# Summing the right operands T1 to T4 of two feed-forward networks from transposed token tiles

## The chip, the core and the metric

The kernel runs on one core of one Trainium2 chip. The metric is the device time of one execution in microseconds (us). Engine names in the profile: PE is TensorE (PEld its weight loads), DVE is VectorE, ACT is ScalarE, POOL is GpSimd, SP is SyncE, which here only issues DMAs. A difference of about 0.3% is what a measurement of this kernel can tell from none.

## The reference

One layer of a hybrid decoder, on 1024 tokens of 1024 channels, in float32:

```python
h = h + 0.5 * swiglu(rmsnorm(h, ffn1_norm), ffn1_w_gate, ffn1_w_up, ffn1_w_down)
...                                    # mixer: four mLSTM heads, eight attention heads
h = h + 0.5 * swiglu(rmsnorm(h, ffn2_norm), ffn2_w_gate, ffn2_w_up, ffn2_w_down)
...                                    # gated per-layer embedding
out = rmsnorm(h)

def swiglu(x, w_gate, w_up, w_down):   # w_gate, w_up: 1024 x 2816, w_down: 2816 x 1024
    return (jax.nn.silu(x @ w_gate) * (x @ w_up)) @ w_down
```

The change touches the first step of both networks: the normalized tokens, transposed, become the right operands of `x @ w_gate` and `x @ w_up`.

## The kernel before

Tokens are handled in eight tiles of 128. Each float32 product is made of three products of a rounded part (`hi`) and a rest (`lo`), in a format that TensorE takes at full rate; `split_from` (line 100) makes both: ScalarE casts the source to `hi`, VectorE subtracts `hi` from the source to get `lo`.

`x @ w_gate` and `x @ w_up` are made by pairs of 128 output columns, as 2 x 2 blocks in Winograd's form: seven block products instead of eight, each of 12 matmuls of 128x512. For this, x transposed is cut in four blocks of 512 channels by 512 tokens: B11 and B21 are the two halves of the channels for the first 512 tokens (tiles 0 to 3), B12 and B22 those for the last 512 (tiles 4 to 7). The right operands are B11, B21, B22 and four sums: T1 = B12 - B11, T2 = B22 - T1, T3 = B22 - B12, and T4 = T2 - B21 with its sign turned. The order of the products in the first pair of columns is g1 u1 g2 u2 g5 g3 u5 u3 g6 g7 g4 u6 u7 u4 (g for gate, u for up): 1 takes B11, 2 B21, 5 T1, 3 B22, 6 T2, 7 T3, 4 T4.

`wino_normer` (line 174) takes one token tile after another. `step(i)` normalizes tile i (a square with a row sum on ScalarE at line 114, a small step on VectorE and GpSimd, and a scaling of 128x1024 on VectorE at line 117) and then calls `finish` for the tile before. For tiles 0 to 3 `finish` transposes both halves with four TensorE transposes each into a PSUM tile (`wino_put`, line 162) and splits them into B11 and B21. The rows of these tiles are kept for tiles 4 to 7: in the first network in SBUF (tag `xk`, four buffers), in the second in DRAM (`xnD`, stored at line 193, loaded at line 196). For tiles 4 to 7 `finish` transposes B22's part, forms the sums on untransposed rows (line 209, two of them on GpSimd, two on VectorE), transposes T1's part, and stores T2, T3 and T4, still as rows, in DRAM (`tD`, line 218). In the second network the two transposes of a tile use PSUM tiles `tr` (two buffers), in the first `pt`, which share five PSUM buffers with the products `pp`.

After the last tile, `ffn` (line 516) loads T2, T3 and T4 (line 546, 1 MB each) into the places of their `lo` parts. Then `wino_rest` (line 222) runs once between products: after the product g3 for T2, after u5 for T3, after u3 for T4. It transposes 16 blocks of 128x128 into four PSUM tiles and splits them. Next come the products that use T2, T3 and T4.

In the first network the token tiles are taken between products of `p @ w_ple_proj` (an order written out as a string at line 1390); in the second, inside the product with `w_out` (`out_f`, line 1288), one tile for every 24 matmuls. Weights are prepared (loaded, summed, split) by `prep` up to three products ahead, and all DMAs go through the queue of SP in order. Within each engine, the order of the instructions is laid out by a scheduler when the kernel is built; it need not be that of the source.

Of the kernel before, what the change touches and what calls it, by code (L numbers as in the profile page):

```python
# [9 lines left out]
F32 = mybir.dt.float32  # L10
# [14 lines left out]
# pairs of dff tiles, and the order of the seven block products of a Winograd form  # L25
# [4 lines left out]
class Net:  # L30
# [26 lines left out]
    def raw_cols(self, w, c0):  # L57
        """128 columns of a [1024, N] weight: row k * 128 + p at [p, k]."""
        r = self.rp.tile([P, KT, P], F32, tag="raw", name="raw")
        self.nc.sync.dma_start(out=r, in_=w[:, c0:c0 + P].rearrange("(k p) n -> p k n", p=P))  # L60
        return r
# [6 lines left out]
    def split(self, raw, pool=None, tag="w", aside=False):  # L68
        """raw = hi + lo, both in float32r."""
# [7 lines left out]
    def split2(self, raw, aside=False):  # L77
        """The two halves of k of a weight tile, each (hi, lo)."""
        return [self.split(raw[:, 4 * j:4 * j + 4, :], aside=aside) for j in range(2)]
# [13 lines left out]
    def mm3(self, out, ahi, alo, bhi, blo, first, last):  # L93
        """out (+)= a.T @ b with a = ahi + alo and b = bhi + blo."""
# [5 lines left out]
    def split_from(self, hi, lo, src, aside=False):  # L100
        """src (PSUM or SBUF) = hi + lo; aside: on GpSimd (SBUF only)."""
# [8 lines left out]
    def norm_rows(self, src, gain, dst):  # L110
        """dst = RMSNorm(src) * gain for 128 tokens; dst also takes the squares."""
# [7 lines left out]
    def xunit(self):  # L119
        """Four k tiles by 512 columns, (hi, lo)."""  # L120
        return tuple(self.xp.tile([P, 4, 512], F32R, tag=t, name=t) for t in ("xhi", "xlo"))

    def new_xt(self):
        """[half of the tokens][half of the k tiles] -> (hi, lo)"""
        return [[self.xunit() for _ in range(2)] for _ in range(2)]

    def normer(self, src, gain, dst):
        """RMSNorm of one token tile after another, transposed and split into dst(i) -> (hi, lo).
        Returns step(i), which takes token tile i and finishes the one before; step.rows(i) only takes it,
        step.next() only finishes the oldest."""  # L130
# [31 lines left out]
    def wino_put(self, B, name, rows, i):  # L162
        """512 columns of token tile i, transposed, into a right operand."""
# [6 lines left out]
        c = (i % 4) * P  # L170
        hi, lo = B[name]
        self.split_from(hi[:, :, c:c + P], lo[:, :, c:c + P], pt)

    def wino_normer(self, src, gain, B, rows, bufs):
        """RMSNorm of one token tile after another into the right operands of the seven products
        (x transposed: rows k < 512 and k >= 512, columns t < 512 and t >= 512, Winograd's form).
        Three operands wait in DRAM for wino_rest. step(i) takes token tile i and finishes the one
        before, step.last() finishes the last."""
# [3 lines left out]
        def step(i):  # L182
            if i < 4 and bufs[2]:
                xn = rows.tile([P, D], F32, tag="xk", name="xn", bufs=bufs[2])
# [7 lines left out]
            elif i < 4 and not kept:  # L192
                nc.sync.dma_start(out=self.xnD[:, i, :], in_=xn)
# [7 lines left out]
        def finish():  # L201
            i, xn, o = queue.pop(0)
            a, b = xn[:, 0:512], xn[:, 512:1024]
            if i < 4:
                self.wino_put(B, "B11", a, i)
                self.wino_put(B, "B21", b, i)
                return
            oa, ob = o[:, 0:512], o[:, 512:1024]
            sub = lambda d, x, y, e=nc.vector: e.tensor_tensor(out=d, in0=x, in1=y, op=ALU.subtract)
            t3 = rows.tile([P, 512], F32, tag="t3", name="t3", bufs=bufs[1])  # L210
            self.wino_put(B, "B22", b, i)
            sub(t3, b, a, nc.gpsimd)
            sub(a, a, oa)
            self.wino_put(B, "T1", a, i)
            sub(oa, b, a)
            sub(ob, ob, oa, nc.gpsimd)
            for n, t in enumerate((oa, t3, ob)):
                nc.sync.dma_start(out=self.tD[:, n, i - 4, :], in_=t)
# [3 lines left out]
    def wino_rest(self, B, name):  # L222
        """One of the operands that wait in DRAM, through its place for lo."""
        hi, lo = B[name]
        pts = []
        for i in range(4):
            pts.append(B["ps"].tile([P, 512], F32, tag="pp", name="pt", bufs=5).rearrange("p (a b) -> p a b", a=4))
            for j in range(4):
                self.nc.tensor.transpose(pts[i][:, j, :], lo[:, i, j * P:(j + 1) * P].bitcast(F32), self.ident)
        for i, pt in enumerate(pts):  # L230
            self.split_from(hi[:, :, i * P:i * P + P], lo[:, :, i * P:i * P + P], pt)

    def swiglu(self, B, w_gate, w_up, pools):
        """hidD = silu(x @ w_gate) * (x @ w_up), transposed, by pairs of dff tiles; the products of a
        pair (2 x 2 blocks: dff tile, half of k, half of the tokens) in Winograd's form with seven
        block products, each of three float32r products."""
# [3 lines left out]
        def pair(m, which, s):  # L240
            """Appends the seven products of the dff tiles m, m + 1."""
# [13 lines left out]
            # the first pair's tile a is loaded again for the sums  # L255
# [18 lines left out]
            def slot(r, c):  # L274
                """Where block (dff tile r, token half c) is put together."""
# [7 lines left out]
            def out(r, c, x, y, t):  # L283
                """Block (r, c) is x + y."""
# [8 lines left out]
            def hidden(r, c):  # L293
                """The left operands of the product with w_down: A11 = H00, A12 = H10, A21 = H01, A22 = H11
                (H: dff tile, half of the tokens), S1 = A21 + A22, S2 = S1 - A11, S3 = A11 - A21, S4 = A12 - S2."""
# [1215 lines left out]
```

## Time and profile before

| What | Value |
|---|---|
| Median of 3 runs | 2029.75 us (2027.75 to 2033.62) |
| Span of the profiled execution | 2033.1 us |
| Time of the profiled execution | not given beside its span |
| TensorE busy | 1982.7 us, 98% of the span |
| VectorE busy | 1408.4 us, 69% |
| ScalarE busy | 856.9 us, 42% |
| GpSimd busy | 135.9 us, 7% |
| DMA | 252.62 MB, mean 124 GB/s |
| The first network's token tiles and first products | 0 to 85 us of the span |
| The same of the second network | 1240 to 1320 us |

A median of the runs is a time of the whole execution; the span goes from the first to the last instruction of one profiled execution, 3.35 us more than the median here. Busy times are sums over the whole span, so an engine's share says little on one stage; the windows and timelines further down show the two stages.

### The profile page before, as it was taken

Reading aid. Unit: us, or ns where it says so; the run is one execution under the profiler, and the core shown is the slowest. Engines: PE = TensorE matmul, PEld = TensorE weight load, DVE = VectorE, ACT = ScalarE, POOL = GpSimd, SP = SyncE. Lnnn points to the kernel's source line nnn. Section 1 sums busy time; section 2 is a strip of 40 time slices with the busy share of each in tenths; the row PEclk is TensorE's granted clock in tenths of the full one; section 3 lists DMA queues with packets and bytes.
Section 4 is the critical chain, followed back from the end, with each engine's and each line's share of the span. In section 5 each row is a group of like instructions: output and inputs, shape, how many; then the busy total and the mean of one; then the engine's idle time right before and its main releaser. Section 6 shows DMA issues by size and latency. Waiting matters only on the chain. (4 is left out here: it accounts for less than half of the span.)

```text
span 2033.1 us, 25588 instructions
## 1 busy us (share of the span) xinstructions
PE 1982.7 (98%) x9251; PEld 1618.8 (80%) x9251; DVE 1408.4 (69%) x2425; ACT 856.9 (42%) x1634; POOL 135.9 (7%) x148
## 2 busy tenths in 40 slices
PE   7999999999999999999999999999999999999998
PEld 6788888888888787788788777788888888888786
DVE  6966766777877683655565665877777777886766
ACT  6433333334445443435565642433333333444443
POOL 2000000000000110121110411100000000000011
PEclk9999999999999999999999999999999999999999
DMA  7623322338432331122112538533223237633422
GB/s 284 207 89 104 112 96 95 104 112 310 149 101 99 111 86 53 42 95 53 53 54 78 190 122 289 197 106 112 94 94 124 89 99 243 234 104 102 131 70 86
DMA packets 205359, 252.62 MB, mean 124 GB/s; under 512 B 12632, under 2 KB 138096, under 8 KB 204464
## 3 DMA queue, kind: packets, MB, share of 16 engines
q1 hardware_dynamic: 205232, 250.99, 37.8%
q8 instruction: 72, 1.18, 0.2%
q14 instruction: 55, 0.45, 0.1%
HBM read 172.18 MB, written 74.58 MB: 121 GB/s over the span
## 5 line engine op out<-in xcount | busy, mean ns | idle before, releaser
L96 PE MATMUL pp<-xhi,whi 128*128 128x512 f32 x704 | 275.6, 391 | 0.5 <-DVE s L272 0.5
L98 PE MATMUL pp<-xhi,wlo 128*128 128x512 f32 x704 | 274.1, 389 | 0.8 <-DVE wlo L103 0.8
L97 PE MATMUL pp<-xlo,whi 128*128 128x512 f32 x704 | 274.7, 390 | 0.0
L102 ACT CAST whi<-raw 128x512 fp32r<-128x512 f32 x180 | 111.3, 621 | 257.4 <-PE pp L97 177.2
L102 ACT CAST whi<-S 128x512 fp32r<-128x512 f32 x176 | 109.5, 622 | 240.8 <-PE pp L97 186.2
L96 PE MATMUL dn<-xhi,whi 128*128 128x512 f32 x528 | 205.7, 390 | 0.1
L97 PE MATMUL dn<-xlo,whi 128*128 128x512 f32 x528 | 205.5, 389 | 0.0
L98 PE MATMUL dn<-xhi,wlo 128*128 128x512 f32 x528 | 205.1, 389 | 0.0
L102 ACT CAST whi<-ar 128x512 fp32r<-128x512 f32 x132 | 82.3, 623 | 183.3 <-PE dn L97 174.8
L98 PEld LDWEIGHTS pp<-xhi,wlo 128*128 128x128 f32 x704 | 132.3, 188 | 29.2 <-DVE wlo L103 1.2
L96 PEld LDWEIGHTS pp<-xhi,whi 128*128 128x128 f32 x704 | 132.3, 188 | 29.1 <-DVE s L272 0.8
L97 PEld LDWEIGHTS pp<-xlo,whi 128*128 128x128 f32 x704 | 132.3, 188 | 27.7 <-DVE xlo L103 0.3
L103 DVE TENSOR_TENSOR wlo<-raw,whi 128x512 fp32r<-128x512 f32 x162 | 110.5, 686 | 59.7 <-ACT whi L102 46.7
L103 DVE TENSOR_TENSOR wlo<-S,whi 128x512 fp32r<-128x512 f32 x176 | 120.1, 682 | 25.8 <-ACT whi L102 25.7
L103 DVE TENSOR_TENSOR wlo<-ar,whi 128x512 fp32r<-128x512 f32 x132 | 90.7, 687 | 63.9 <-ACT whi L102 63.8
L96 PEld LDWEIGHTS dn<-xhi,whi 128*128 128x128 f32 x528 | 99.1, 188 | 21.0 <-DVE t L272 0.5
L98 PEld LDWEIGHTS dn<-xhi,wlo 128*128 128x128 f32 x528 | 99.1, 188 | 20.7
L97 PEld LDWEIGHTS dn<-xlo,whi 128*128 128x128 f32 x528 | 99.1, 188 | 20.6
L272 DVE TENSOR_TENSOR p<-pp,p 128x512 f32<-128x512 f32 x88 | 60.6, 689 | 74.9 <-PE pp L98 74.9
L107 POOL TENSOR_TENSOR r<-v,mhalf 128x1 f32<-128x1 f32 (+1 forms) x56 | 43.9, 784 | 909.6 <-DVE v L116 756.1
L96 PE MATMUL pj<-xhi,whi 128*128 128x512 f32 x248 | 102.6, 414 | 0.1
L97 PE MATMUL pj<-xlo,whi 128*128 128x512 f32 x248 | 97.5, 393 | 0.0
(350 smaller groups left out, 4515.0 us busy)
## 6 DMA issues: line engine op xcount, KB each, us to landing
ar<-hidD SPq DMA_DIRECT2D x60, 512.0 KB, 3.6
hidD<-t SPq DMA_DIRECT2D x110, 256.0 KB, 3.4
raw<-in_ffn_w_gate_dram SPq DMA_DIRECT2D x46, 512.0 KB, 3.9
raw<-in_ffn_w_up_dram SPq DMA_DIRECT2D x46, 512.0 KB, 3.7
raw<-in_w_in_dram SPq DMA_DIRECT2D x24, 512.0 KB, 3.9
hidD<-x SPq DMA_DIRECT2D x44, 256.0 KB, 3.1
ar<-hidD SPq DMA_DIRECT2D x32, 256.0 KB, 2.9
w<-in_ffn_w_down_dram SPq DMA_DIRECT2D x8, 1024.0 KB, 11.1
```

Of the source, the lines that this page charges most:

```text
L96: mm(out, ahi, bhi, start=first, stop=False)
L97: mm(out, ahi, blo, start=False, stop=False)
L98: mm(out, alo, bhi, start=False, stop=last)
L102: self.nc.scalar.copy(out=hi, in_=src)
L103: (self.nc.gpsimd if aside else self.nc.vector).tensor_tensor(out=lo, in0=src, in1=hi.bitcast(F32), op=ALU.subtract)
L107: self.nc.gpsimd.tensor_tensor(out=r, in0=v, in1=self.mhalf[:, :v.shape[-1]], op=ALU.pow)
L272: add = lambda d, x, y: nc.vector.tensor_tensor(out=d, in0=x, in1=y, op=ALU.add)
```

## The change

`wino_normer` now transposes both halves of every token tile first (`turned`, in place of `wino_put`). For tiles 0 to 3 B11 and B21 are split from the transposed tiles in PSUM as before, and ScalarE also copies both to SBUF, over the normalized rows; it is these transposed tiles that are kept, and in the second network stored in `xnD`, now in `finish`. For tiles 4 to 7 T1 and T2 are formed on VectorE from PSUM and the kept tiles, T3 (as T2 - B11) and T4 on GpSimd from SBUF. T1 is split from SBUF. T2, T3 and T4 go to DRAM already transposed, T2 from the tile of the normalized rows, in pieces of 128 columns (512 bytes) instead of rows of 512 (2 KB). `wino_rest` has no transposes any more; it splits the loaded operand in place, in four blocks of 512 columns. The tag `t3` and its buffer are gone, so `bufs` has one entry less.

```diff
-    def wino_put(self, B, name, rows, i):
+    def turned(self, B, rows):
         if "ps" in B:
             pt = B["ps"].tile([P, 512], F32, tag="pp", name="pt", bufs=5).rearrange("p (a b) -> p a b", a=4)
         else:
             pt = self.tr()
         for j in range(4):
             self.nc.tensor.transpose(pt[:, j, :], rows[:, j * P:(j + 1) * P], self.ident)
-        c = (i % 4) * P
-        hi, lo = B[name]
-        self.split_from(hi[:, :, c:c + P], lo[:, :, c:c + P], pt)
+        return pt
...
         def step(i):
-            if i < 4 and bufs[2]:
-                xn = rows.tile([P, D], F32, tag="xk", name="xn", bufs=bufs[2])
+            if i < 4 and bufs[1]:
+                xn = rows.tile([P, D], F32, tag="xk", name="xn", bufs=bufs[1])
                 kept.append(xn)
...
-            elif i < 4 and not kept:
-                nc.sync.dma_start(out=self.xnD[:, i, :], in_=xn)
             elif i >= 4:
                 o = self.rp.tile([P, D], F32, tag="raw", name="xo")
                 nc.sync.dma_start(out=o, in_=self.xnD[:, i - 4, :])
...
         def finish():
             i, xn, o = queue.pop(0)
-            a, b = xn[:, 0:512], xn[:, 512:1024]
+            c = (i % 4) * P
+            put = lambda name, src: self.split_from(B[name][0][:, :, c:c + P], B[name][1][:, :, c:c + P], src)
+            quad = lambda t, b: t[:, b * 512:b * 512 + 512].rearrange("p (a c) -> p a c", a=4)
+            pa = self.turned(B, xn[:, 0:512])
+            pb = self.turned(B, xn[:, 512:1024])
+
+            a, b = quad(xn, 0), quad(xn, 1)
             if i < 4:
-                self.wino_put(B, "B11", a, i)
-                self.wino_put(B, "B21", b, i)
+                put("B11", pa)
+                put("B21", pb)
+                nc.scalar.copy(out=a, in_=pa)
+                nc.scalar.copy(out=b, in_=pb)
+                if not bufs[1]:
+                    nc.sync.dma_start(out=self.xnD[:, i, :], in_=xn)
                 return
-            oa, ob = o[:, 0:512], o[:, 512:1024]
+            oa, ob = quad(o, 0), quad(o, 1)
             sub = lambda d, x, y, e=nc.vector: e.tensor_tensor(out=d, in0=x, in1=y, op=ALU.subtract)
-            t3 = rows.tile([P, 512], F32, tag="t3", name="t3", bufs=bufs[1])
-            self.wino_put(B, "B22", b, i)
-            sub(t3, b, a, nc.gpsimd)
-            sub(a, a, oa)
-            self.wino_put(B, "T1", a, i)
-            sub(oa, b, a)
-            sub(ob, ob, oa, nc.gpsimd)
-            for n, t in enumerate((oa, t3, ob)):
-                nc.sync.dma_start(out=self.tD[:, n, i - 4, :], in_=t)
+            sub(a, pa, oa)
+            put("B22", pb)
+            sub(b, pb, a)
+            put("T1", a)
+            sub(oa, b, oa, nc.gpsimd)
+            sub(ob, ob, b, nc.gpsimd)
+            for n, t in enumerate((b, oa, ob)):
+                nc.sync.dma_start(out=self.tD[:, n, :, c:c + P], in_=t)
...
     def wino_rest(self, B, name):
         hi, lo = B[name]
-        pts = []
-        for i in range(4):
-            pts.append(B["ps"].tile([P, 512], F32, tag="pp", name="pt", bufs=5).rearrange("p (a b) -> p a b", a=4))
-            for j in range(4):
-                self.nc.tensor.transpose(pts[i][:, j, :], lo[:, i, j * P:(j + 1) * P].bitcast(F32), self.ident)
-        for i, pt in enumerate(pts):
-            self.split_from(hi[:, :, i * P:i * P + P], lo[:, :, i * P:i * P + P], pt)
+        for k in range(4):
+            self.nc.scalar.copy(out=hi[:, k, :], in_=lo[:, k, :].bitcast(F32))
+            self.nc.vector.tensor_tensor(out=lo[:, k, :], in0=lo[:, k, :].bitcast(F32), in1=hi[:, k, :].bitcast(F32), op=ALU.subtract)
...
-        N.ffn(h, ffn1_norm[0], ffn1_w_gate[0], ffn1_w_up[0], ffn1_w_down[0], norms, hook, (3, 1, 4), True)
+        N.ffn(h, ffn1_norm[0], ffn1_w_gate[0], ffn1_w_up[0], ffn1_w_down[0], norms, hook, (3, 4), True)
...
-    N.ffn(h, ffn2_norm[0], ffn2_w_gate[0], ffn2_w_up[0], ffn2_w_down[0], norms, hook, (2, 1, 0), release=late.close)
+    N.ffn(h, ffn2_norm[0], ffn2_w_gate[0], ffn2_w_up[0], ffn2_w_down[0], norms, hook, (2, 0), release=late.close)
```

The rest of the diff takes comments and docstrings out of the source, with the lines kept, and changes no instruction.

## Rows read from the trace of the kernel before

**Rows 1.** The page's first part: busy us, share of the span and instructions of each engine (PE is TensorE, PEld its weight loads, DVE VectorE, ACT ScalarE, POOL GpSimd).

```profile
PE 1982.7 (98%) x9251; PEld 1618.8 (80%) x9251; DVE 1408.4 (69%) x2425; ACT 856.9 (42%) x1634; POOL 135.9 (7%) x148
```

**Rows 2.** Busy time by stretches of 10 us, at the start of the first feed-forward network (two) and of the second (one). In order: the stretch in us from the span's start, its length, and for each engine the busy us and in brackets its instructions; then the granted clock of TensorE as a share of full speed, the busy share of the DMA engines, and GB/s.

```profile
60.00:70.00 10.00, 7.71 (x40) 5.74 (x39) 8.23 (x14) 4.66 (x9) 0.00 (x0) 1.00 0.90 335
...
70.00:80.00 10.00, 10.00 (x62) 8.70 (x61) 9.48 (x17) 6.14 (x12) 0.00 (x0) 1.00 0.37 113
...
1290.00:1300.00 10.00, 8.30 (x37) 6.56 (x35) 7.99 (x14) 4.45 (x7) 0.00 (x0) 1.00 1.00 351
```

**Rows 3.** TensorE's timeline at the start of the first network. Columns of a timeline: start in us, duration in us (of all instructions merged into the row, if several), engine, line, operation, output and input by the program's names, tile, how many instructions, and in square brackets the idle time of that engine just before, with what ended it.

```profile
51.61 2.34 PE L169 MATMUL pt<-ident,xn 128*128 128x128 f32 x16
...
57.58 0.50 PE L97 MATMUL pp<-xlo,whi 128*128 128x512 f32 x1
...
61.96 0.50 PE L98 MATMUL pp<-xhi,wlo 128*128 128x512 f32 x1 [0.80 <-DVE wlo L103]
...
64.12 0.39 PE L98 MATMUL pp<-xhi,wlo 128*128 128x512 f32 x1
...
66.00 1.94 PE L229 MATMUL pt<-ident,T2lo 128*128 128x128 f32 x16 [1.48 <-DMA T2lo<-tD]
...
75.03 1.91 PE L229 MATMUL pt<-ident,T4lo 128*128 128x128 f32 x16
...
76.70 0.48 PE L96 MATMUL pp<-T2hi,whi 128*128 128x512 f32 x1
...
82.38 0.40 PE L96 MATMUL pp<-T4hi,whi 128*128 128x512 f32 x1
```

**Rows 4.** TensorE's timeline at the start of the second network, columns as in rows 3.

```profile
1286.71 0.66 PE L169 MATMUL pt<-ident,xn 128*128 128x128 f32 x4 [0.78 <-DVE xn L209]
...
1297.92 0.39 PE L98 MATMUL pp<-xhi,wlo 128*128 128x512 f32 x1
...
1300.30 3.25 PE L229 MATMUL pt<-ident,T2lo 128*128 128x128 f32 x16 [1.99 <-DMA T2lo<-tD]
...
1312.67 0.48 PE L96 MATMUL pp<-T2hi,whi 128*128 128x512 f32 x1
...
1318.35 0.40 PE L96 MATMUL pp<-T4hi,whi 128*128 128x512 f32 x1
```

**Rows 5.** A stretch of 2 us in the second network, columns as in rows 2.

```profile
1302.00:1304.00 2.00, 2.00 (x10) 1.90 (x9) 1.23 (x3) 1.47 (x3) 0.00 (x0) 0.50 0.23 68
```

**Rows 6.** VectorE's timeline in the first network, columns as in rows 3.

```profile
50.03 1.42 DVE L209 TENSOR_TENSOR xn<-xn 128x512 f32<-128x512 f32 x2 [1.41 <-POOL t L209]
...
55.64 1.89 DVE L103 TENSOR_TENSOR xlo<-pt,xhi 128x512 fp32r<-128x512 f32 x3 [0.60 <-ACT xhi L102]
...
67.70 2.48 DVE L103 TENSOR_TENSOR T2lo<-pt,T2hi 128x512 fp32r<-128x512 f32 x4 [1.19 <-PE pt L229]
...
72.32 2.48 DVE L103 TENSOR_TENSOR T3lo<-pt,T3hi 128x512 fp32r<-128x512 f32 x4 [0.34 <-ACT T3hi L102]
...
77.12 2.48 DVE L103 TENSOR_TENSOR T4lo<-pt,T4hi 128x512 fp32r<-128x512 f32 x4
```

**Rows 7.** Groups of VectorE's instructions from 56 to 80 us, one row for a line, names and shape: count, busy us, mean ns of one, and idle time before them with what ended it.

```profile
L252 DVE TENSOR_TENSOR S<-S,raw 128x512 f32<-128x512 f32 x4 | 2.8, 688 | 0.6 <-DMA raw<-in_ffn_w_gate_dram 0.3 <-DMA raw<-in_ffn_w_up_dram 0.3
...
L252 DVE TENSOR_TENSOR S<-raw 128x512 f32<-128x512 f32 x4 | 2.7, 685 | 0.3 <-DMA raw<-in_ffn_w_up_dram 0.3
```

**Rows 8.** VectorE's timeline in the second network, columns as in rows 3.

```profile
1297.08 0.69 DVE L252 TENSOR_TENSOR S<-S,raw 128x512 f32<-128x512 f32 x1 [1.14 <-DMA raw<-in_ffn_w_up_dram]
...
1303.00 2.48 DVE L103 TENSOR_TENSOR T2lo<-pt,T2hi 128x512 fp32r<-128x512 f32 x4 [0.77 <-ACT T2hi L102]
...
1308.17 2.48 DVE L103 TENSOR_TENSOR T3lo<-pt,T3hi 128x512 fp32r<-128x512 f32 x4 [0.32 <-ACT T3hi L102]
...
1313.02 2.47 DVE L103 TENSOR_TENSOR T4lo<-pt,T4hi 128x512 fp32r<-128x512 f32 x4
```

**Rows 9.** Timelines of the first network, one row of GpSimd and two of VectorE (the normalization of a token tile, beside a GpSimd subtraction and without one), columns as in rows 3.

```profile
30.05 1.28 POOL L209 TENSOR_TENSOR t<-xn 128x512 f32<-128x512 f32 x1
...
30.12 2.28 DVE L117 SCALAR_TENSOR_TENSOR xn<-h,r,gain 128x1024 f32<-128x1024 f32 x1 [1.92 <-POOL r L107]
...
25.93 1.28 DVE L117 SCALAR_TENSOR_TENSOR xn<-h,r,gain 128x1024 f32<-128x1024 f32 x1
```

**Rows 10.** DMA issues: output and input, engine, how many, KB of each, median us from issue to landing.

```profile
ar<-hidD SPq DMA_DIRECT2D x60, 512.0 KB, 3.6
...
raw<-in_ffn_w_gate_dram SPq DMA_DIRECT2D x46, 512.0 KB, 3.9
...
tD<-xn SPq DMA_DIRECT2D x8, 256.0 KB, 4.1
...
tD<-xo SPq DMA_DIRECT2D x8, 256.0 KB, 2.2
```

**Rows 11.** ScalarE's copies of 128x512 from PSUM to SBUF in the first 60 us (count, then minimum, median and maximum ns), and a stretch of 30 us with the columns of rows 2.

```profile
L599 ACT COPY pp<-pp x16: 586/600/639, 14.2 to 48.2; 128x512 f32<-128x512 f32 x16
...
20.00:50.00 30.00, 28.10 (x145) 22.79 (x144) 21.81 (x33) 20.53 (x42) 11.56 (x11) 1.00 0.74 267
```

**Rows 12.** Timeline rows of the second network: TensorE's transposes of token tile 4, and ScalarE's squares of token tile 6. Columns as in rows 3.

```profile
1265.32 1.03 PE L169 MATMUL tr<-ident,xn 128*128 128x128 f32 x8
...
1273.85 1.06 ACT L114 ACTIVATE xn<-h 128x1024 f32<-128x1024 f32 x1 [0.83 <-DMA tD<-t]
```

## The prediction

> **What bounds the kernel now.** I read the page's first part first, then the stretches around the two places that the change touches: the start of the first feed-forward network (FFN1, up to 85 us of the span) and of the second (FFN2, 1240 to 1320 us). TensorE is busy 98% of the span [rows 1], so what is worth something here is TensorE's own work and the few waits of TensorE, and nothing that another engine does beside it.
>
> The windows show the three places where that is not so. From 60 to 70 us TensorE has 7.71 busy us of ten, and from 1290 to 1300 us 8.30; VectorE (DVE) has 9.48 from 70 to 80 us, as TensorE has 10.00 [rows 2]. So right behind the stall DVE is nearly full too, and a faster TensorE may find DVE in its way. That is the point on which my sum turns.
>
> TensorE's timeline shows the stall itself. In FFN1 the last matmul of a product starts at 64.12; the 16 transposes of T2 wait 1.48 us more for the load of T2 and start at 66.00; those of T4 start at 75.03 and the next product, the first that uses T2, at 76.70 [rows 3]. FFN2 has the same: 1297.92, a wait of 1.99, 1300.30, and the first product with T2 at 1312.67; there the last tile's T1 transposes waited 0.78 for DVE besides [rows 4]. After the wait of 1.99 the granted clock was 0.50 (1.2 GHz) from 1302 to 1304 [rows 5], which is why those 16 transposes took 3.25 us.
>
> **What goes.** Per network 3 x 16 = 48 transposes in wino_rest (8 per token tile stay). Sixteen take 75.03 to 76.70 = 1.67 us [rows 3], so 96 take 10.0 us of TensorE. With them goes TensorE's wait for the load: the two products that run between the loads (u5, u3) no longer have transposes ahead of them. The ceiling is read from the gap. In FFN1 12.35 us lie between the end of the product at 64.35 (64.12 + 0.23) and the first with T2; two products take 82.38 - 76.70 = 5.68; 6.7 us can go. In FFN2 (1312.67 - 1298.15) - 5.68 = 8.8, and 0.78 for T1. Together 16.3 us.
>
> **What DVE lets through.** The twelve subtractions per network that make the lo parts of T2, T3 and T4 stay: four take 2.48 us [rows 6], from PSUM before and from SBUF after, and SBUF sums of the same size have the same 0.69 us mean [rows 7]. Before, the last of T4 ends at 77.12 + 2.48 = 79.60 and T4's first product starts at 82.38: 2.8 us to spare. In FFN2 1313.02 + 2.47 = 1315.49 against 1318.35: 2.9 [rows 3, 4, 6, 8]. If DVE came no earlier, 2.8 and 2.9 would be all that TensorE gains. DVE comes earlier by idle time that it now has. In FFN2 that is 1.14 + 0.77 + 0.32 = 2.2 us, the second of which is the wait for the old transposes [rows 8]; so 2.9 + 2.2 + 0.8 (T1) = 5.9. In FFN1 0.6 + 0.3 (waits for weights) [rows 7] and 0.34 [rows 6] give 2.8 + 1.2 = 4.0. The 1.19 before T2's first subtraction I don't count: T2's data landed at 66.0 before, and it lands no sooner after, so cast and subtraction start near 67 anyway. The ends: DVE blocks all but the 2.8 and 2.9, or nothing, since DVE can take T4 before sums that are needed later.
>
> **What moves behind the transposes.** B12 - B11 (T1) and B22 - T1 (T2) were DVE work on rows, done before TensorE reached the tile: both of the last pair of sums at 50.03 [rows 6], the transposes at 51.61 [rows 3]. Now both wait for the transposes. In FFN1 the lo part of T1's last tile ends at 55.64 + 1.89 = 57.53 [rows 6] and the product's second matmul starts at 57.58 [rows 3]: nothing to spare. After: the first eight of the 16 transposes end near 52.6; then eight DVE operations of two tiles (8 x 0.62 = 5.0) and two others (1.2) end at 58.8, that is 1.3 late. GpSimd comes on top. It has the same two subtractions per tile, but both now depend on T2 and start just when DVE makes T1's lo part from SBUF. The rows show what that does: DVE's normalization took 2.28 us beside a GpSimd subtraction that started 0.07 before it, 1.28 without one [rows 9]. So 0 to 1.3 us for each of two tiles; I take the middle, 1.3. Of 2.6 us TensorE's 0.80 wait at 61.96 [rows 3] takes up some; 1.8 stay. FFN1: 4.0 - 1.8 = 2.2.
>
> The page SBUF — State Buffer of the Trainium skill (Who interferes with whom) says that a DVE instruction with two SBUF inputs and a GpSimd instruction that reads SBUF exclude each other for the whole instruction, and that one with an input in PSUM is not touched. By that rule both T1 subtractions pay in full or stop GpSimd, and FFN1 gives 0.9, not 2.2; the trace agrees with the rule where it has such a pair (2.28 against 1.28).
>
> In FFN2 T1's last lo part is less pressed: two products of B21 (5.7 us) run between the last tile's transposes and T1's first use, in FFN1 only one. DVE's count there is the same, so I charge nothing; without that cover it would be FFN1's 1.8. T3 was ready early before and is not now; its load follows T2's instead of leading it, which costs nothing as long as T3 lands 2.8 us after T2, and a megabyte took less than that at the rates of these windows (335 to 351 GB/s: 3.0 us, all but equal) [rows 2]. I take zero there, 1 us at worst.
>
> **What is added.** ScalarE copies each of the first four transposed tiles to SBUF: 8 x 0.60 = 4.8 us per network [rows 11]. In FFN1 ScalarE is busy 20.5 of the 30 us from 20 to 50 [rows 11], so they fit; but they hold the PSUM buffers longer, and TensorE waited for such buffers there. 0 to 2 us, I take 0.4, near zero since TensorE has other work between tiles. The tD stores have pieces of 512 bytes, not 2 KB. Weights come in such pieces: 512 KB land in 3.9 us, the 2-KB pieces of hidD in 3.6 [rows 10]. By that an eighth more for 256 KB that took 4.1, some 0.4 us, hidden in FFN2 by the products and inside the 67 us above in FFN1. The xnD store of FFN2 waits for the copies now, one tile later, with the load of the next h row behind it on the SP queue; it waited for a normalization before, which ends about when the tile before it has been transposed and copied, so zero, and 1 us for the six tiles at worst.
>
> **Sum.** 2.2 + 5.9 - 0.4 = 7.7 us off the profiled span of 2033.1, which gives 2025.4. The page shows no time of its own for that execution; the runs' median is 2029.75, 3.35 below the span, so the same 7.7 off the median gives 2022.0.
>
> **Rivals.**
> *TensorE keeps everything* (16.3 us, 2013.5). For it: swiglu prepares weights three products ahead (8.5 us), so DVE may run late by some us without stopping TensorE, and T4's subtractions can go before sums that are needed later. Against: DVE at 9.48 and T1 with nothing to spare. 0.17.
>
> *DVE gives the gain back.* FFN1 gains nothing (both GpSimd blocks in full, 4.0 - 3.1 = 0.9, and 1.0 more for the copies), FFN2 only 2.9: 3.8 - 0.8 = 3 us, 2026.8. It decides where DVE's idle us before T4 stay idle, because DVE now waits for T2's load itself, with weights queued behind it, where TensorE waited before. The section of SBUF — State Buffer in the Trainium skill named above speaks for this one. 0.27.
>
> *Slower: the normalization loses its buffers.* T2 is now stored from xn itself, and GpSimd reads it there, so a buffer comes free only when the store has landed, not at the transposes. FFN2 has two such buffers: tile 6 starts at 1273.85 and needs tile 4's, whose transposes begin at 1265.32 [rows 12]. After: 1.0 for transposes, 2.0 for three DVE steps, 2.2 to 4.1 for a store [rows 10], so free at 1270.5 to 1272.4, and 1.4 to 3.3 to spare. It decides if the chain is over 8.5 us long; then each of six tiles is late by the same amount, and from 2.4 us each (14 us) the kernel is over 6 us slower: 2036. FFN1 has three buffers, so it is less tight. 0.08.
>
> That the transposes stay is no case: wino_rest issues none.
>
> **Numbers.** My forecast (FFN1 1 to 5, FFN2 4.5 to 7) has 0.48; its own range is 2018 to 2025. The range for 8 in 10 reaches into both neighbours: 2014.5 to 2029.5. A measurement can tell about 0.3% (6.1 us, so 2023.7) from no change. Faster by more: all of the first rival (0.17) and most of the forecast (0.42), 0.59. Within: the rest of it (0.06), the second rival (0.27), and a little of the third, 0.34. Slower: 0.07.
>
> **What would show it.** Right: TensorE's wait for T2 gone, no transposes of T2lo, T3lo, T4lo; the granted clock at 1.00 right through FFN2's start; T4's first product at 80 in FFN1 and 1312 in FFN2, and DVE without idle time before it. T1's product in FFN1 should start its second matmul near 60, with DVE's xlo named. Wrong: a wait of TensorE for T2's or T3's subtraction over 2 us, DVE waiting for DMA with weights behind it, or ScalarE's squares in FFN2 waiting for a tD store. The rest of the kernel should run as before, only earlier; if the order of instructions elsewhere moved, that would be outside this sum.

## The result, and the profile after

The change makes the kernel slower by about 7 us: 2037.24 us (median of 6 runs, 2036.19 to 2038.3) against 2030.26 (6 runs, 2027.75 to 2033.62), ratio 1.0033, 95% interval 1.0021 to 1.0045. I had forecast 2022.0, with a range that ended at 2029.5. The profiled execution of after took 2038.3 us and its span is 2036.5.

The page's first part, engine by engine (answers to [rows 1]):

```profile
PE 1977.3 (97%) x9155; PEld 1610.0 (79%) x9155; DVE 1411.0 (69%) x2425; ACT 863.7 (42%) x1650; POOL 138.7 (7%) x148
```

Exactly the 96 transposes are gone, but TensorE is busy only 5.4 us less, where the transposes were priced at 10.0, and no less than in a second profile of the kernel before (1977.3, the run `e1_before_again` below). The windows, columns as in [rows 2], show one reason: behind its waits TensorE was granted a lower clock, so the same matmuls took longer.

```profile
50.00:60.00 10.00, 6.74 (x34) 4.87 (x32) 8.84 (x13) 4.63 (x7) 7.11 (x5) 0.93 0.94 290
60.00:70.00 10.00, 8.38 (x27) 6.11 (x26) 9.16 (x13) 2.74 (x5) 2.35 (x2) 0.73 1.02 318
...
1290.00:1300.00 10.00, 7.92 (x33) 5.61 (x32) 8.69 (x11) 4.64 (x7) 4.45 (x3) 1.00 0.71 203
1300.00:1310.00 10.00, 5.64 (x21) 3.51 (x19) 7.21 (x12) 4.61 (x9) 0.00 (x0) 0.89 1.04 395
1310.00:1320.00 10.00, 9.94 (x34) 7.68 (x34) 9.62 (x17) 5.11 (x10) 0.00 (x0) 0.77 0.21 64
```

TensorE's timeline in the two networks' first products, columns as in [rows 3] and [rows 4]:

```profile
58.45 0.73 PE L96 MATMUL pp<-xhi,whi 128*128 128x512 f32 x1 [2.10 <-ACT xhi L102]
59.59 0.79 PE L97 MATMUL pp<-xlo,whi 128*128 128x512 f32 x1 [0.41 <-DVE xlo L103]
61.27 0.80 PE L98 MATMUL pp<-xhi,wlo 128*128 128x512 f32 x1 [0.89 <-DVE wlo L103]
66.92 0.50 PE L96 MATMUL pp<-xhi,whi 128*128 128x512 f32 x1 [0.73 <-ACT whi L102]
74.76 0.40 PE L96 MATMUL pp<-T2hi,whi 128*128 128x512 f32 x1
80.36 0.40 PE L96 MATMUL pp<-T4hi,whi 128*128 128x512 f32 x1
...
1297.59 0.50 PE L96 MATMUL pp<-xhi,whi 128*128 128x512 f32 x1 [1.25 <-ACT whi L102]
1302.38 0.50 PE L96 MATMUL pp<-xhi,whi 128*128 128x512 f32 x1 [0.88 <-ACT whi L102]
1309.15 0.79 PE L96 MATMUL pp<-xhi,whi 128*128 128x512 f32 x1 [3.48 <-ACT whi L102]
1314.77 0.39 PE L96 MATMUL pp<-T2hi,whi 128*128 128x512 f32 x1
1320.36 0.40 PE L96 MATMUL pp<-T4hi,whi 128*128 128x512 f32 x1
```

No wait for T2 is left. In its place TensorE waits for T1 (58.45) and above all for weights, whi and wlo. In FFN1 the first product with T2 comes at 74.76, between the two profiles of the kernel before (76.70 and 74.15); in FFN2 it starts 34.1 us after the network's first product, where the two of before have 32.9 and 31.4.

Why the weights are late in FFN2 is read from the timelines of SP's queue, VectorE and ScalarE of after, columns as in [rows 3]:

```profile
1294.66 2.06 SPq L223 DMA_DIRECT2D tD<-xo  x2
1296.83 0.45 SPq L60 DMA_DIRECT2D raw<-in_ffn_w_up_dram  x1
1297.46 0.58 SPq L547 DMA_DIRECT2D T2lo<-tD  x1
1298.31 0.33 SPq L298 DMA_DIRECT2D hidD<-t  x1
1298.77 0.66 SPq L60 DMA_DIRECT2D raw<-in_ffn_w_up_dram  x1
...
1300.98 0.69 DVE L253 TENSOR_TENSOR S<-raw 128x512 f32<-128x512 f32 x1 [2.10 <-DMA raw<-in_ffn_w_up_dram]
...
1304.03 2.18 ACT L231 CAST T2hi<-T2lo 128x512 fp32r<-128x512 f32 x4 [1.71 <-DMA T2lo<-tD]
...
1304.74 1.90 DVE L232 TENSOR_TENSOR T2lo<-T2lo,T2hi 128x512 fp32r<-128x512 f32 x3 [1.09 <-ACT T2hi L231]
1306.55 0.68 DVE L253 TENSOR_TENSOR S<-S,raw 128x512 f32<-128x512 f32 x1
```

The last T3 and T4 (the two stores from xo) go out at 1294.66, the up weights and T2's load only after them. VectorE waits 2.10 for the weights, then 1.09 for T2, and the next weight sum (1306.55) stands behind T2's split. That is what TensorE's 3.48 waits for. Before, these loads were issued at 1286.33, 1291.90 and (T2) 1292.33.

To see where time goes over the whole span, I cut it at TensorE's matmul groups, by their first or last start in the trace: the start to the last product with T4 (FFN1's products), from the last transpose of the mixer's attention to FFN2's first product (its normalization), on to FFN2's last product with T4, and on to the first product of the gate behind FFN2 (called FFN2's down product). What lies between FFN1's products and the attention's end differs by 1.2 us between before and after and is left out. In us, before and after as means of two profiles each (the second ones are of the runs `e1_before_again` and `e4_ring` below), the others from one. The two profiles of before differ by 2.6, 0.4, 1.5 and 0.4 us in these four stretches and by 3.2 in what is left out, so a difference of 2 or 3 us in one stretch is not clear of noise:

| Kernel | FFN1 products | FFN2 normalization | FFN2 products | FFN2 down product |
|---|---|---|---|---|
| before | 477.7 | 75.9 | 434.5 | 214.3 |
| after | 478.2 | 78.1 | 436.1 | 215.9 |
| only wino_rest new | 474.9 | 75.5 | 428.7 | 218.4 |
| after, no T3 and T4 sums | 475.5 | 76.1 | 427.5 | 215.2 |

### The profile page after: what moved, and what is told of

It reads as the page before. It is cut to its first block, busy times and chain, and to the rows that moved or that the text cites. A ratio compares the mean times of both kernels' runs of the same rounds, so it can differ in the third digit from the quotient of the medians.

```text
span 2036.5 us, 25405 instructions
## 1 busy us (share of the span) xinstructions
PE 1977.3 (97%) x9155; PEld 1610.0 (79%) x9155; DVE 1411.0 (69%) x2425; ACT 863.7 (42%) x1650; POOL 138.7 (7%) x148
## 6 DMA issues: line engine op xcount, KB each, us to landing
w<-in_ffn_w_down_dram SPq DMA_DIRECT2D x8, 1024.0 KB, 10.4
```

## The experiments

All were timed against the kernel before on the same chip. The last column is (ratio - 1) x 2030; its interval is 2 us to either side for most runs and up to 3.6. Differences between runs are differences of that column, and less certain than each of the two.

| Run | Median us | Ratio, 95% interval | us against before |
|---|---|---|---|
| e1_before_again | 2029.60 | 0.9999, 0.9989 to 1.0008 | -0.2 |
| e2_rest_only | 2023.95 | 0.9972, 0.9960 to 0.9983 | -5.7 |
| e3_finish_only | 2042.51 | 1.0060, 1.0044 to 1.0076 | +12.2 |
| e4_ring | 2036.31 | 1.0032, 1.0021 to 1.0044 | +6.5 |
| e5_no_gpsimd | 2023.78 | 0.9969, 0.9958 to 0.9979 | -6.3 |
| e11_aside | 2033.84 | 1.0020, 1.0011 to 1.0029 | +4.1 |
| e8_three_bufs | 2034.05 | 1.0021, 1.0011 to 1.0030 | +4.3 |
| e10_rows_first | 2032.24 | 1.0010, 1.0000 to 1.0019 | +2.0 |
| e6_dve_subs | 2036.40 | 1.0025, 1.0013 to 1.0037 | +5.1 |
| e12_dve_three | 2032.69 | 1.0014, 1.0005 to 1.0024 | +2.8 |
| e14_half_three | 2032.86 | 1.0014, 1.0004 to 1.0023 | +2.8 |
| e13_before_nogps | 2028.61 | 0.9997, 0.9988 to 1.0006 | -0.6 |
| e17_early_sums | 2028.41 | 0.9995, 0.9986 to 1.0004 | -1.0 |
| e18_early_rows | 2027.50 | 0.9994, 0.9984 to 1.0005 | -1.2 |
| e16_dve_aside | 2030.12 | 1.0000, 0.9991 to 1.0010 | 0.0 |
| e15_xo_own | 2038.66 | 1.0048, 1.0031 to 1.0065 | +9.7 |
| e19_pool_queue | 2033.32 | 1.0011, 1.0001 to 1.0021 | +2.2 |
| e20_pool_queue_gps | 2041.13 | 1.0060, 1.0042 to 1.0077 | +12.2 |

**The two halves of the change.** `e1_before_again` is the kernel before, unedited. `e2_rest_only` is the kernel before with the new `wino_rest` and two PSUM tiles that nothing uses, allocated behind it to bring the turn of the five buffers back; `e3_finish_only` is the kernel after with the old `wino_rest`, `e4_ring` the kernel after with the two unused tiles.

```diff
             for n, name in enumerate(("T2", "T3", "T4")):
                 products(6 + n)
                 self.wino_rest(B, name)    # e2: the new one in before; e3: the old one in after
+            for _ in range(2):             # e4 (and e2)
+                B["ps"].tile([P, 512], F32, tag="pp", name="turn", bufs=5)
             down = self.down(h, w_down, hook)
```

> The kernel before, unchanged, for a second profile of it. The span of its first profile is 2033.1 us; a time lies 1.8 us over its span (2038.3 against 2036.5 in the kernel after), so that execution took 2034.9, more than each of its six timed runs (2027.8 to 2033.6). If that execution was an untypically long one, the new span is near 2028.5 and the trace shows which wait of the first is missing; the half clock behind the wait for T2 in the second network (1.2 us in the first profile) is the candidate. If it was typical, the span is again near 2033 and the loss of the change is half of what the medians say.

> The kernel before with the new wino_rest alone: no transposes of T2, T3, T4, which stay untransposed, so T2 to T4 are other numbers; two unused PSUM tiles keep the ring of five where it was. Theory 1 (the rearranged finish costs more than the transposes gave): the removal alone gains what I had worked out for DVE's limit without the later T1, 4.0 + 5.1 = 9 us, so 2021; at least the 5.7 us that T4 had to spare. Theory 2 (the removal itself brings nothing, since T2's load and DVE behind it bind): within 2 us of before.

> The kernel after with the old wino_rest: the sums formed from transposed tiles, and 48 transposes per network made again (of data already transposed, so T2 to T4 are other numbers). Theory 1: the rearranged finish alone costs the 7 us of the change plus what the removal gains, 12 to 16 us: 2042 to 2046. Theory 2: 7 us over before, 2037. If the loss were the rotation of the PSUM ring, which this kernel doesn't have, it would be within 4 us of before.

> The kernel after with two unused PSUM tiles before the product with w_down in both networks, so that the ring of five buffers is where it was before the change (12 allocations fewer move it by two places). In the profile of after TensorE's first matmul of that product waits 1.1 and 1.6 us for DVE's sum on the last product, in the one of before it does not. If the ring's place is the cause, both waits go and the time falls by 2.7 us to 2034.5; if not, they stay and it is 2037.

The halves add up: -5.7 + 12.2 = +6.5, against the change's 6.7. So dropping the transposes gained, as I thought, if less than the 9.1 I reckoned for it, and the rearranged `finish`, charged with 2.2 (1.8 for T1 and 0.4), cost some 12. The unused tiles changed nothing. That is no test of the buffers' turn, since tiles that nothing uses may not take a turn at all; what the wait at the down product (below) comes from stays open.

**GpSimd's two sums.**

```diff
-            sub(oa, b, oa, nc.gpsimd)      # e5: both gone
-            sub(ob, ob, b, nc.gpsimd)
+            sub(t3, b, oa, nc.gpsimd)      # e11: both into a spare tile t3
+            sub(t3, ob, b, nc.gpsimd)
```

> The changed kernel without GpSimd's two sums per token tile: T3 and T4 are left out, the stores write what the tile xo holds. The rearranged finish costs 12.6 us by the runs so far; four causes are open. A, late stores: GpSimd's sums start only behind T2, their stores stand at the head of SP's queue, and loads of weights and of T2 wait behind them; then the 7 us come back and a little more, 2027 to 2031. B, GpSimd and VectorE keep each other from SBUF: the same 2027 to 2031, and VectorE's subtractions of 1.77 us are 0.69 again. C, T1's sum behind the transposes: 2034 to 2037, no more than 2 us faster than the change. D, the buffers of the normalized rows that T2's store holds: 2033 to 2036, since stores land earlier by only 3 us.

> The changed kernel with GpSimd's two sums per token tile still made, of the same operands, but into a spare tile that no store reads; so T3 and T4 are left out of the result and the stores of xo don't wait for GpSimd. It parts A from B. A (late stores): as without the sums, 2027 to 2031. B (GpSimd and VectorE exclude each other at SBUF): as the change, 2035 to 2038, with subtractions of 1.77 us still there. C and D: within 2 us of the change.

Without the two sums all of the 12 us is gone (13.0): copies, small pieces, T1's place and T2's store, all of which `e5_no_gpsimd` keeps, leave it no slower than `e2_rest_only`. That is more than any of the four causes in the expectation allowed. With the sums made but not stored 10.4 of them are back, between what A and B said; the stores' wait for GpSimd is 2.6.

The 10.4 have two parts that `e11_aside` doesn't separate, since GpSimd still reads xo there, and late. The waits of SP's queue in FFN2 (1270 to 1303 us: in all, how many, the longest) show that the weights' loads, line 60, wait until it has. In `e5_no_gpsimd` they don't wait for xo at all.

```profile
SPq L60 <- POOL t L215: 8.7, 3, 3.0
```

The other part is VectorE's own time. FFN1 shows it alone, since the kept tiles have buffers of their own there. From 54 to 71 us VectorE runs the same instructions in the same order in both kernels, so their timelines show what GpSimd does to it. First three rows of VectorE without the sums (`e5_no_gpsimd`):

```profile
54.81 0.69 DVE L103 TENSOR_TENSOR xlo<-xn,xhi 128x512 fp32r<-128x512 f32 x1 [0.66 <-ACT xhi L102]
58.42 0.68 DVE L251 TENSOR_TENSOR S<-raw 128x512 f32<-128x512 f32 x1
59.02 0.68 DVE L288 TENSOR_TENSOR t<-t,s 128x512 f32<-128x512 f32 x1
```

The same three with the sums (`e11_aside`), one with an input in PSUM between them, and GpSimd's rows:

```profile
54.68 1.30 DVE L103 TENSOR_TENSOR xlo<-xn,xhi 128x512 fp32r<-128x512 f32 x1 [0.73 <-ACT xhi L102]
55.90 0.68 DVE L215 TENSOR_TENSOR xn<-pt,xn 128x512 f32<-128x512 f32 x1
58.90 1.15 DVE L255 TENSOR_TENSOR S<-raw 128x512 f32<-128x512 f32 x1
59.97 1.76 DVE L292 TENSOR_TENSOR t<-t,s 128x512 f32<-128x512 f32 x1
...
51.12 5.99 POOL L215 TENSOR_TENSOR t<-xn 128x512 f32<-128x512 f32 x4 [2.69 <-DVE xn L215]
57.95 3.23 POOL L215 TENSOR_TENSOR t<-xn 128x512 f32<-128x512 f32 x2 [0.84 <-DVE xn L215]
```

Three subtractions from SBUF are 2.2 us longer in sum, those from PSUM are not (55.90, 0.68, inside GpSimd's 51.12 to 57.11), and the first product with T2 is 2.6 us later (75.7 against 73.1). The section that the prediction named from the Trainium skill's SBUF — State Buffer (Who interferes with whom) says just this of SBUF and PSUM inputs, and the rows agree. In FFN2, where both parts come in, the sums aside make the normalization 1.7 us longer (77.8 against 76.1) and the products 4.7 (432.2 against 427.5); the stores add 3.9 there (436.1) and nothing in FFN1.

**On VectorE instead.** `e6_dve_subs` makes both sums on VectorE, `e16_dve_aside` too but into the spare tile, `e13_before_nogps` takes the sums out of the kernel before.

```diff
-            sub(oa, b, oa, nc.gpsimd)
-            sub(ob, ob, b, nc.gpsimd)
+            sub(oa, b, oa)                 # e6; e16: sub(t3, b, oa), sub(t3, ob, b)
+            sub(ob, ob, b)
```

> The changed kernel with T3's and T4's sums of each token tile on VectorE instead of GpSimd; nothing is left out. Without these sums the time was 2023.8, with them on GpSimd 2037.2. If what cost 13.4 us is GpSimd's part in it (VectorE kept from SBUF beside it, and stores that wait for it), moving 8 x 0.6 us per network to VectorE costs at most 2 x 4.8 us: 2024 to 2033, and I expect 2029. If the cost were that the sums come late at all, 2034 or more.

> The changed kernel with T3's and T4's sums made on VectorE into a spare tile that no store reads; T3 and T4 are left out of the result. Beside the run without the sums (2023.8) only VectorE's 2 x 8 subtractions are added, beside the run with the sums on VectorE (2036.4) only the wait of the stores is gone. If what costs is VectorE's time in the bound stretch: 2030 to 2034. If it is that xo is stored late and holds a buffer that weights need: 2024 to 2028.

> The kernel before without GpSimd's two sums per token tile: T3 and T4 are left out, their stores write the tile xo. It tells whether GpSimd's sums cost the kernel before anything too, where they did not wait for T2's transposes. If the cost is where the change puts them, 2028 to 2031, as before. If GpSimd beside VectorE costs the same wherever it runs, 2017 to 2022.

Here the theory that GpSimd itself is at fault fell: on VectorE the sums cost 11.4, all but as much. Of these 5.1 are the late stores. The other 6.3 are VectorE's time (16 subtractions of 0.6 are 9.6 us, of which some found room) together with the weights' wait for VectorE's late reads of xo, 5.9 us of SP's queue in `e16_dve_aside`; the two are not taken apart. TensorE's timeline of `e6_dve_subs`, its longest wait in each network:

```profile
63.66 0.79 PE L96 MATMUL pp<-xhi,whi 128*128 128x512 f32 x1 [6.73 <-ACT whi L102]
...
1308.51 0.80 PE L96 MATMUL pp<-xhi,whi 128*128 128x512 f32 x1 [4.14 <-ACT whi L102]
```

It is the weights again, whose sums queue on VectorE behind the tile's; without the sums the first of these waits is 4.38 (`e5_no_gpsimd`) and the second is not there. And before the change the same sums cost 0.6, which is nothing that can be told.

**Their place, and T1's.** `e17_early_sums` makes GpSimd's sums of untransposed rows ahead of the transposes; `e10_rows_first` makes T1's there and leaves GpSimd's late; `e18_early_rows` does both.

```diff
+            sub(t3, b, a, nc.gpsimd); sub(ob, ob, oa, nc.gpsimd)   # e17, e18
+            sub(a, a, oa)                                          # e10, e18
             pa = self.turned(B, xn[:, 0:512])
             pb = self.turned(B, xn[:, 512:1024])
...
-            sub(a, pa, oa)                                         # e10, e18
-            sub(oa, b, oa, nc.gpsimd); sub(ob, ob, b, nc.gpsimd)   # e17, e18
```

> The changed kernel with T1's sum made on the rows ahead of the transposes again, B22 transposed first and T1 split from PSUM, as before; T2's sum then mixes rows and a transposed tile, so T1 to T4 hold other numbers than they should, at the same cost. C (T1's sum behind the transposes, which I charged with 1.8 us): 4 to 6 us come back in the first network and 1 to 3 in the second, 2029 to 2032. A, B, D: within 2 us of the change, 2035 to 2038.

> The changed kernel with as many sums on GpSimd, but made of the untransposed rows ahead of the transposes, as before, so that they wait for nothing of the tile's own T2: T3 from the two halves of the rows into a tile of its own, T4 in the tile xo. T3 and T4 then mix layouts and hold other numbers than they should, at the same cost. The place theory (the same two sums cost 1 us ahead of the transposes and 13 behind them, because there they lie beside or ahead of VectorE's chain for T1 and hold xo's buffer): 2024 to 2029. The load theory (VectorE has no room for GpSimd beside it in this kernel at all): 2033 to 2037.

> As the run before (GpSimd's sums of rows ahead of the transposes), and T1's sum made on the rows ahead of the transposes too, B22 transposed first; only T2's sum still waits for a transposed tile. T1 to T4 hold other numbers than they should, at the same cost. What is left of the change then are ScalarE's copies, the stores in pieces of 512 bytes, the later store to xnD and T2's store from xn. If these cost nothing, as I charged them (0.4), the time is that of the kernel before with the new wino_rest: 2022 to 2026. If they are a cost of their own: 2027 or more. If T1's place alone costs something beside early sums, this run is faster than the one before by that.

Place is the larger part: the same sums on the same engine, made early, give back 7.7 of the 13.0. T1's sum made early gives back 4.7 while GpSimd's come late, and nothing that can be told beside early ones (-1.2 against -1.0). But 5.3 is not back, and its cause is open. The FFN2 normalization takes 78.7 us in `e17_early_sums`, where two of ScalarE's squares wait for T2's store from xn. That wait alone doesn't explain it: `e5_no_gpsimd`, whose normalization takes 76.1, has nearly the same one. Their timelines, `e17_early_sums` first:

```profile
1284.20 1.06 ACT L114 ACTIVATE xn<-h 128x1024 f32<-128x1024 f32 x1 [7.40 <-DMA tD<-xn]
...
1277.93 1.06 ACT L114 ACTIVATE xn<-h 128x1024 f32<-128x1024 f32 x1 [6.84 <-DMA tD<-xn]
```

In `e18_early_rows` no square waits for a store, and the normalization takes 80.2; its products of FFN2 are the fastest of all runs (426.0), and the stretch behind them the slowest (219.7). But its profile is of the longest of its ten executions (2033.74 us, where the median is 2027.50), so little can be built on its stretches.

**Buffers and queues.**

```diff
-    N.ffn(..., hook, (2, 0), release=late.close)                       # e8, e12, e14, e19, e20
+    N.ffn(..., hook, (3, 0), release=late.close)
-                o = self.rp.tile([P, D], F32, tag="raw", name="xo")   # e15
+                o = rows.tile([P, D], F32, tag="xo", name="xo", bufs=1)
-                nc.sync.dma_start(out=self.tD[:, n, :, c:c + P], in_=t)
+                nc.gpsimd.dma_start(out=self.tD[:, n, :, c:c + P], in_=t)   # e19, e20
```

> The changed kernel with three buffers for the normalized rows in the second network instead of two; nothing is left out. D (the square of the normalization waited 6.99 us for the store of T2 from xn): TensorE's waits for xn of 0.3 and 1.3 us in the product with w_out go, and with them 2 to 4 us, 2033 to 2035. A, B, C: those waits are of VectorE or GpSimd, and the time stays within 1.5 us of the change, 2036 to 2038.

> The changed kernel with T3's and T4's sums on VectorE, and three buffers for the normalized rows in the second network instead of two; nothing is left out. Three buffers alone gave 3.2 us. If the buffers were held because GpSimd's sums delayed T2's neighbours on the queue, they give nothing more here: the time of the sums on VectorE alone, within 1 us. If they are a cause of their own, 2 to 3 us less than that.

> The changed kernel with T3's sums on VectorE and T4's left on GpSimd, and three buffers for the normalized rows in the second network; nothing is left out. If GpSimd's cost goes by its number of instructions beside VectorE, half of it stays: 2 to 6 us slower than with both sums on VectorE and three buffers. If VectorE's own time is the bound in these stages, it is up to 2 us faster than that.

> The changed kernel with a buffer of its own for xo in the second network, instead of one of the four that it shares with the loads of weights; nothing is left out. There is room for one only, so a tile's xo is loaded when that of the tile before has been stored. If late weights behind held buffers are what the second network loses (the up weights issued at 1296.8 and 1298.8, against 1281.3 and 1285.6 without the sums), 3 to 6 us come back, less what the single buffer costs the normalization: 2031 to 2036. If not, 2036 to 2042.

> The changed kernel with T3's and T4's sums on VectorE and three buffers for the normalized rows in the second network (2032.7), and the stores of T2, T3 and T4 issued from GpSimd's DMA queue instead of SP's; nothing is left out. If the second network loses its time because stores that wait at the head of SP's queue keep back the weights behind them: the up weights are issued by 1290 instead of 1296, and 3 to 6 us go, 2026 to 2030, which would be a little faster than the kernel before. If it is because the weights' buffers are held until the stores have landed, or because T2's load waits for the last store anyway: within 2 us of 2032.7.

> The changed kernel with its sums on GpSimd and three buffers for the normalized rows (2034.05), and the stores issued from GpSimd's queue; nothing is left out. SP's queue is free of stores here too, but GpSimd issues three DMAs between its own sums and the small step of the normalization. Queue at fault: 2029 to 2032. Buffers or the last store at fault: 2032 to 2036, or more if issuing delays the normalization.

A third buffer for xn is worth 2.4 us with the sums on GpSimd and 2.3 with them on VectorE, so it seems a cause of its own, though each difference is about as large as its noise. Splitting the sums between the engines changed nothing, which neither branch of the expectation had. xo's own buffer made it 3.0 us worse, and settles nothing: there was room for one only, and the tile's own chain then waited for it (TensorE 5.9 us for T1's xhi, and no longer for weights). Moving the stores to GpSimd's queue freed SP's, but the first up weights were issued at 1288.86, where `e12_dve_three` has 1289.97; that was worth 0.6. So it is not the stores' place at the head of SP's queue that keeps the weights back. The waits of SP's queue in `e19_pool_queue`, 1270 to 1303 us, show what does: the landing of the stores from xo, whose buffers the weights need.

```profile
SPq L60 <- DMA tD<-xo: 12.6, 2, 6.4
...
SPq L547 <- DMA tD<-xn: 4.1, 1, 4.1
```

What is late next is seen in the timelines of SP's queue, ScalarE and VectorE of `e19_pool_queue`:

```profile
1293.52 0.34 SPq L547 DMA_DIRECT2D T2lo<-tD  x1
...
1298.99 2.18 ACT L231 CAST T2hi<-T2lo 128x512 fp32r<-128x512 f32 x4 [3.75 <-DMA T2lo<-tD]
...
1299.64 0.69 DVE L232 TENSOR_TENSOR T2lo<-T2lo,T2hi 128x512 fp32r<-128x512 f32 x1 [3.79 <-ACT T2hi L231]
...
1301.45 0.68 DVE L253 TENSOR_TENSOR S<-S,raw 128x512 f32<-128x512 f32 x1
```

T2's load waits for the landing of T2's own last store, from xn, whatever the queue, and both engines wait for it with a weight sum behind. With the sums on GpSimd, issuing the stores from GpSimd as well made it 7.9 slower than `e8_three_bufs`. No version that leaves nothing out beat the kernel before; the best of them lie 2 to 3 us above it.

## Why the prediction was wrong

**What goes, and what VectorE lets through: right.** I reckoned 4.0 us in FFN1 and 5.1 in FFN2 without T1's wait (2.9 + 2.2). With only `wino_rest` new the products of the two networks are 2.8 and 5.8 shorter, which is the same within the noise of a stretch. That the gain would stop at VectorE and not at the 16.3 was right too, and the 16.3 were read from a long execution (its span is 2033.1 us, that of the second profile 2024.5): in `e1_before_again` FFN1's wait for T2 is 0.27 us instead of 1.48, and in FFN2 the clock stayed at 1.00 behind the wait (2.19), so that T2's 16 transposes took 1.94 instead of 3.25. I didn't see that 4.1 us of it go again behind FFN2's products: TensorE then starts the down product with a wait that the kernel before does not have. TensorE's timeline of `e2_rest_only`:

```profile
1702.95 0.77 PE L96 MATMUL dn<-xhi,whi 128*128 128x512 f32 x1 [2.08 <-DVE t L268]
```

The granted clock is 0.83 there from 1700 to 1710. In after the same wait is 1.55. Why it comes is open.

**What moves behind the transposes, FFN1: right in kind, small in size.** T1's second matmul starts at 59.59 with xlo named (I said near 60), and T4's first product at 80.36 (I said 80). That second agreement says little, since `e1_before_again` has it at 79.83 with the old transposes. Against `e2_rest_only` the rearranged step costs FFN1's products 3.3 us, where I charged 1.8 and 0.4.

**FFN2: the step that failed.** I wrote that T1 is less pressed there and "so I charge nothing", and of T2's to T4's loads only that their order changes. Against `e2_rest_only` the step cost 2.6 us in FFN2's normalization and 7.4 in its products. I followed T1, which did have its cover, and not the two sums on GpSimd. For FFN1 I had seen that they now depend on T2, and charged what they do to T1's split; for FFN2 they got no price, nor did their stores in either network. They are the same two as before, and without them the change would have been worth 6.3 us. But they had been made on rows, ahead of the transposes, where they cost nothing that can be told; now they wait for T2 and come last in a tile's chain. There they stretch VectorE's weight sums (FFN2's S at 1293.41 took 1.77 us, 0.69 without GpSimd), hold xo, one of the four buffers that weights are loaded into, and put off the last stores. That xo shares its buffers with the weights is in the code, and no step of mine used it. The traces point at the weights more than at T2's late load. Counted from FFN2's first product, the second up load is issued at 12.1 us in before, 18.1 in after, 10.4 in `e5_no_gpsimd` and 12.1 in `e17_early_sums`; T2's load at 12.5, 16.8, 15.1 and 17.0. So `e17_early_sums` has T2 as late as after, and yet FFN2's products take 429.0 us there, 7.1 less. How much the held buffer costs by itself, beside the stretched sums, no run separates.

**VectorE gives the gain back, the second rival,** named the mechanism: VectorE waits for T2's load itself, with weights queued behind it (1.09 at 1304.74, and TensorE's 3.48). Its floor was too high: I let FFN2 keep 2.9.

**The slower rival** had the sign, and its mechanism is there, at one tile. ScalarE's timeline of after, the square of the last tile ([rows 12] show that of tile 6):

```profile
1283.14 1.06 ACT L114 ACTIVATE xn<-h 128x1024 f32<-128x1024 f32 x1 [6.99 <-DMA tD<-xn]
```

Of the squares, only the last tile's waits for a store, a third buffer gave 2.4 us, not 14, and `e5_no_gpsimd` has the same wait (6.84) without the loss. So it is at most a part of the loss and not its cause.

**The clock.** I expected 1.00 through FFN2's start, since the wait for T2 would go. Other waits took its place, and the clock was 0.77 from 1310 to 1320 and in FFN1, where it had been 1.00, 0.73 from 60 to 70.

**What is added.** ScalarE's copies and the 512-byte pieces cost nothing that shows once the sums are out (-6.3 against -5.7). Beside GpSimd's sums, early ones too, up to 4.5 us remain (`e18_early_rows` against `e2_rest_only`) that I have not taken apart. Two small slips of the sum moved it by no more than 0.3 us: 3.9 against 3.6 us is a twelfth more and not an eighth, and a megabyte at 335 to 351 GB/s takes 3.0 to 3.1 us, which is not less than the 2.8 that T3 had.

## What to carry to other kernels

When a sum is moved behind another step, follow all that hangs on it to its last store, and not only the operand that is needed first: who reads it, whose buffer it holds, and which loads stand behind its store. Work that costs nothing where an engine idles costs time where that engine is the bound, and moving it to another engine helps little if the place stays. Cost each half of a change alone; here the half with the work was off by 3 us and the half that only moved work by 10.

## What the runs showed of the hardware

A GpSimd subtraction between SBUF tiles and a VectorE one lengthen each other: in after VectorE's took up to 1.77 us instead of 0.69, and a pair of GpSimd's 3.25 (at 50.56 us) where it took 2.84 earlier (42.37 us). VectorE's subtractions with an input in PSUM kept 0.68. A store of 256 KB issued by GpSimd kept GpSimd for 0.75 to 0.93 us in `e19_pool_queue`, against 0.36 to 0.62 for SP in after.
